# A mixed mLSTM and attention layer on one core: the last normalisation as weighted rows with a shift from row-group products, and a third block of rows as row products

## The chip, the cores and the metric

The kernel is one program on one core of a Trainium2 chip. The metric is the device time of one execution in microseconds (us), the median of three runs. Engines are TensorE (PE; its loads of stationary operands are PEld), VectorE (DVE), ScalarE (ACT), GpSimd (POOL) and SyncE (SP, which issues nearly all DMAs here). SBUF is the memory the engines work on, PSUM the one that TensorE writes its sums to.

## What is computed

One inference step of a hybrid decoder layer, for 512 prompt tokens and 32 sample tokens (8 sequences of 4), 2048 wide. Only its end is touched: the output projection, the residual and the normalisation.

```python
def _layernorm(x, w, b):
    xf = x.astype(jnp.float32)
    mu = jnp.mean(xf, axis=-1, keepdims=True)
    var = jnp.mean(jnp.square(xf - mu), axis=-1, keepdims=True)
    return (xf - mu) * lax.rsqrt(var + LN_EPS) * w.astype(jnp.float32) + b.astype(jnp.float32)
...
    y = (jax.nn.sigmoid(g_m) * jnp.einsum('btc,cd->btd', br_m, w_proj_m)
         + jax.nn.sigmoid(g_a) * jnp.einsum('btc,cd->btd', br_a, w_proj_a))
    out = jnp.einsum('btc,cd->btd', y, w_out)
    return _layernorm(DN_ALPHA * x + out, ln_w, ln_b).astype(x.dtype)
```

## The kernel before

Input projection, attention, the mLSTM state updates and two inner projections come first and take some 2285 us; nothing of them is changed. All products are made of values split in two (`hilo`, `split`: a rounded high part on ScalarE, the rest on VectorE), three products for each pair: high by high, low by high, high by low.

The last stage multiplies the gated sum `y` (tiles `yh`, `yl`, 2048 rows by T = 544 tokens) with `w_out`. Weight columns go in 16 groups `ct` of 128. For groups 0 to 12 the weights are the stationary operand and the tokens stream through: 16 inner steps x 3 products x two pieces of 256 and 288 tokens. The result stands transposed, columns by tokens; ScalarE copies it to `ot` (`evac`), TensorE turns it back in pieces of 128 tokens (`add_residual`, by `ident`), and VectorE adds it to `z`, which holds the prompt's rows as 4 blocks of 128 tokens (`zs` holds the 32 sample rows, folded to 128 partitions by 512). After each fourth group, `stats` collects mean and variance of a quarter of each row (`bn_stats`).

For the last three groups (`G3 = 3`, 13 to 15) only tokens 256 to 543 are done that way: 48 products of 288 columns each. For token blocks 0 and 1 the roles are swapped in `rows_of(t)`: the tokens of the block are the stationary operand, the 384 weight columns stream through in pieces of 256 and 128, 96 products a block, and the sum comes out as rows, so that one operation of VectorE (`add_rows`, L1692) adds them, with no transpose behind.

`moments(t)` makes a block's mean and variance, and GpSimd raises the variance to the power -1/2 (L1660). `finish(t)` then works in pieces: VectorE makes (z - mean) x `lw` (L1677); either VectorE makes that times the power plus `lb` (L1682), or ScalarE multiplies and GpSimd adds (L1679, L1680); SP sends the piece out. Blocks 2 and 3 and the samples are finished beside `rows_of(0)`, block 0 beside `rows_of(1)`, block 1 last in smaller pieces (`LAST`). `load_ln` loads `ln_w` and `ln_b`, each copied to all 128 partitions, and in the samples' folded form (`lwq`, `lbq`: the 32 partitions of row group q hold quarter q).

The instructions of an engine run in the order of its queue. A scheduler with its own model of times sets this order from the program, ahead of time; where `manual_schedule` names TensorE, its instructions stay in the order in which the code issues them. Elsewhere in the kernel there is already a product on four row groups: in the state update (L1133) four products of 32 rows, each with its own `tile_position`, follow one another, and VectorE reads the four results (L1136). fp32 products, as with `ident` or `cq`, run at full precision.

## Time and profile before

| | us |
|---|---|
| median of 3 runs | 2511.45 (2511.23 to 2512.54) |
| profiled execution | 2510.62 |
| its span | 2508.8 |
| TensorE busy | 2468.9 (98%) |
| VectorE busy | 1778.4 (71%) |
| ScalarE busy | 1211.9 (48%) |
| GpSimd busy | 366.5 (15%) |

The profile shows one execution. Its page gives the busy time of each engine and the chain of work that ended last (TensorE makes up 89% of it); the trace behind it gives every instruction with start and duration. Products on TensorE are pipelined, so that the duration of one overlaps the next: the price of one in a row of them is the distance between starts.

### The profile page before, as it was taken

How to read it: one execution, taken by the hardware profiler on the slowest of the kernel's cores; microseconds unless marked ns; L12 is line 12 of the kernel's file. 1: busy time of each engine (PE TensorE's matmuls, PEld its weight loads, DVE VectorE, ACT ScalarE, POOL GpSimd, SP SyncE). 2: the span in 40 equal slices, each digit the busy share in tenths (PEclk: the TensorE clock that was granted, in tenths of full speed). 3: DMA queues.
4: the chain of work that ended last, by engine and by line, in shares of the span. 5: the costliest groups of instructions: out<-in, count | busy, mean ns of one | idle time of the engine just before them, and what ended most of it. 6: DMA issues, size and time to landing. Idle time of an engine off the chain costs nothing.

```text
span 2508.8 us, 48732 instructions
## 1 busy us (share of the span) xinstructions
PE 2468.9 (98%) x19711; PEld 2408.4 (96%) x19711; DVE 1778.4 (71%) x2608; ACT 1211.9 (48%) x1965; POOL 366.5 (15%) x442
## 2 busy tenths in 40 slices
PE   8999999999999999999999999999999999999997
PEld 8999999999999999999999999999999998999997
DVE  7867777777777777788777888877766655766336
ACT  4447667667667665433434445444533323344221
POOL 2111111111111111221111222100000011110002
PEclk9999999999999999999999999999999999999998
DMA  6566666666666655477585784874555467987332
GB/s 194 136 167 149 160 157 153 152 153 156 150 158 152 153 135 152 118 245 238 168 276 170 233 251 131 260 239 128 180 167 164 163 207 218 249 207 236 93 102 80
DMA packets 548322, 439.18 MB, mean 175 GB/s; under 512 B 44256, under 2 KB 459280, under 8 KB 547808
## 3 DMA queue, kind: packets, MB, share of 16 engines
q1 hardware_dynamic: 535392, 389.85, 52.8%
q0 software_dynamic: 12704, 46.21, 10.0%
q8 instruction: 155, 2.54, 0.4%
q14 instruction: 71, 0.58, 0.1%
HBM read 302.68 MB, written 90.32 MB: 157 GB/s over the span
## 4 chain that ended last, share of the span: by engine, by line
PE 89%; DMA 3%; DVE 2%; issue 1%; ACT 1%; SPq 0%; POOL 0%; DVEq 0%; ACTq 0%; POOLq 0%
PE bank L634 43%; PE bank L636 21%; PE bank L229 11%; PE sm L1317 2%; PE sum L1128 1%; PE sm L1349 1%; PE sm L1362 1%; PE sm L744 1%; PE sm L784 1%; PE bank L1727 1%; PE sm L774 1%; PE sm L229 1%; DMA d_n<-fr 1%; PE sm L1133 1%; DVE wl L213 1%
## 5 line engine op out<-in xcount | busy, mean ns | idle before, releaser
L212 ACT CAST wh<-raw 128x1024 fp32r<-128x1024 f32 x628 | 657.8, 1048 | 889.1 <-PE bank L634 595.2
L213 DVE TENSOR_TENSOR wl<-raw,wh 128x1024 fp32r<-128x1024 f32 x628 | 778.5, 1242 | 296.2 <-ACT wh L212 293.2
L634 PE MATMUL bank<-xk,wh 128*128 128x272 f32 x2304 | 315.9, 289 | 1.7 <-DVE ev L659 1.7
L614 DVE TENSOR_TENSOR raw<-raw,raw 128x1024 f32<-128x1024 f32 x234 | 297.9, 1273 | 25.4 <-DMA raw<-in_w_proj_m 17.1
L634 PEld LDWEIGHTS bank<-xk,wh 128*128 128x128 f32 x2304 | 297.8, 188 | 5.3 <-issue 2.5
L653 POOL TENSOR_TENSOR ev<-p,ev 128x272 f32<-128x272 f32 x80 | 115.1, 1439 | 564.0 <-ACT ev L652 530.2
L636 PE MATMUL bank<-xk,wl 128*128 128x272 f32 x1152 | 167.1, 287 | 0.0
L636 PEld LDWEIGHTS bank<-xk,wl 128*128 128x128 f32 x1152 | 153.5, 188 | 0.0
L634 PE MATMUL bank<-n2h,wh 128*128 128x272 f32 x576 | 147.3, 289 | 2.0 <-ACT wh L212 2.0
L634 PE MATMUL bank<-s4h,wh 128*128 128x272 f32 x576 | 148.7, 291 | 0.0
L634 PE MATMUL bank<-s1h,wh 128*128 128x272 f32 x576 | 148.7, 291 | 0.1
L634 PE MATMUL bank<-a11h,wh 128*128 128x272 f32 x576 | 148.0, 289 | 0.0
L634 PE MATMUL bank<-n3h,wh 128*128 128x272 f32 x576 | 147.5, 289 | 0.0
L634 PE MATMUL bank<-a11l,wh 128*128 128x272 f32 x576 | 147.2, 289 | 0.0
L634 PE MATMUL bank<-n3l,wh 128*128 128x272 f32 x576 | 146.9, 288 | 0.0
L634 PE MATMUL bank<-s4l,wh 128*128 128x272 f32 x576 | 146.7, 287 | 0.0
L634 PE MATMUL bank<-s1l,wh 128*128 128x272 f32 x576 | 146.6, 287 | 0.0
L634 PE MATMUL bank<-n2l,wh 128*128 128x272 f32 x576 | 146.6, 287 | 0.0
L612 POOL DMA_DIRECT2D raw<-raw x86 | 74.5, 866 | 403.5 <-DVE raw L614 173.7
L659 DVE SCALAR_TENSOR_TENSOR ev<-bank,ev 128x272 f32<-128x272 f32 x80 | 35.3, 441 | 119.4 <-PE bank L636 119.4
L229 PE MATMUL bank<-bh,wl 128*128 128x272 f32 x512 | 109.9, 291 | 6.3 <-DVE wl L213 6.3
L634 PEld LDWEIGHTS bank<-n2h,wh 128*128 128x128 f32 x576 | 108.3, 188 | 3.2 <-ACT wh L212 2.2
(503 smaller groups left out, 5928.9 us busy)
## 6 DMA issues: line engine op xcount, KB each, us to landing
raw<-in_w_in SPq DMA_DIRECT2D x296, 512.0 KB
raw<-raw POOLq DMA_DIRECT2D x86, 512.0 KB, 4.9
C<-in_state_mlstm_C SPq DMA_DIRECT2D x32, 1024.0 KB
out<-C SPq DMA_DIRECT2D x64, 512.0 KB
raw<-in_w_proj_a SPq DMA_DIRECT2D x32, 512.0 KB
raw<-in_w_proj_m SPq DMA_DIRECT2D x32, 512.0 KB
raw<-in_w_out SPq DMA_DIRECT2D x32, 512.0 KB
d_sgm<-ev SPq DMA_DIRECT2D x16, 272.0 KB
```

The lines of the kernel that those rows point to most:

```text
L212: state["wh"] = A.copy(wh[:], raw[:])
L213: state["wl"] = V.tensor_tensor(out=wl[:], in0=raw[:], in1=r32(wh[:]), op=ALU.subtract)
L229: PE.matmul(ps[ALL, f, 0:w], a[:, kk], b(k, c, w), start=(k == 0 and n == 0), stop=(k == 15 and n == 2))
L612: G.dma_start(out=w[out][:], in_=w[b][:], accum_op=ALU.add)
L614: V.tensor_tensor(out=w[out][:], in0=w[a][:], in1=w[b][:], op=ALU.add)
L634: PE.matmul(ps, wh[:, k], x(p, k), start=(first and k == 0 and p == 0), stop=False, skip_group_check=True)
L636: PE.matmul(ps, wl[:, k], x(0, k), start=False, stop=(k == 7), skip_group_check=True)
L653: G.tensor_tensor(out=c22, in0=p1, in1=c11, op=ALU.subtract)
L659: V.scalar_tensor_tensor(c22, B0, -sc, c22, op0=ALU.mult, op1=ALU.add)
L744: PE.matmul(pp[:, c0 + w0:c0 + 256], qs[a][:, j * 128:j * 128 + 128], kx[:, k0:k0 + 256 - w0], start=(n == 0), stop=(n == 1))
L774: PE.transpose(pt[:, (m - m0_) * 128:(m - m0_) * 128 + 128], s_[:, b, 128:256] if own else s_[:, b + 1, 0:128], ident)
L1317: PE.matmul(pp[:, 0:258], a[:, b * 128:b * 128 + 128], b_[:, b, f], start=(b == 0 and n == 0), stop=(b == 3 and n == 2))
```

## The change

The normalisation is rearranged: (z - m) r w + b becomes (z w) r + (b - m r w). The first factor, z w, is made ahead (`weighted`): for the first three quarters of each row as soon as their statistics are taken, for the last quarter of a block behind its statistics. The second term, the shift, is a product with five inner rows: `sh` holds, for each quarter on its own 32 partitions, the high and low parts of b and w (rows 0 to 4: b high, b low, w high, w low, w high), and `mc` holds 1, 1, and the high, high and low parts of -m r. `shift` fills `mc` for a block on VectorE, `turned` transposes it on TensorE and copies it on ScalarE, and `finish` makes four products of 32 rows by 512 columns, one on each row group, into four banks. VectorE then makes z r + shift, one operation for each quarter. For the very last quarter TensorE adds z r itself by a product with a diagonal matrix of r (`dg`, fp32), and ScalarE copies the result out. `lb` and its 1 MB load are gone; GpSimd keeps only the power.

Block 2 moves to the row products as well: `rows_of` runs for blocks 2, 0 and 1, and the last three groups do 160 columns (block 3 and the samples) in place of 288. The row products and what is put between them (`at2`, `at8`, ...: the inner step ahead of which it is issued) are in program order on TensorE.

```diff
 SLOPES = [float(np.float32(2.0 ** (-8.0 * (h + 1) / AH))) for h in range(AH)]
-C_ID, C_TRI, C_DIST, C_SB, C_M8, C_SM, C_SEL, C_R, C_Q, C_N = 0, 128, 256, 512, 644, 652, 684, 716, 730, 858
+C_ID, C_TRI, C_DIST, C_SB, C_M8, C_SM, C_SEL, C_R, C_Q, C_N = 0, 128, 256, 512, 644, 652, 684, 716, 730, 862
...
     c[:, C_Q:C_Q + 128] = np.where(tok[:, None] == tok[None, :], 0.25, 0.0)
+    j = p % 32
+    for n, rows in enumerate(((0, 1), (2, 3, 4), (0, 2, 4), (1, 3))):
+        c[:, C_Q + 128 + n] = np.isin(j, rows)
...
     lw = d1.tile([128, D], F32, name="lw")
-    lb = d1.tile([128, D], F32, name="lb")
+    sh = d1.tile([128, 512], F32R, name="sh")
+    shw = [d1.tile([128, 512], F32, name=nm("shw")) for _ in range(2)]
+    mc = [d1.tile([128, 4, 32], F32R, name=nm("mc")) for _ in range(2)]
+    mT = [d1.tile([128, 128], F32R, name=nm("mT")) for _ in range(2)]
+    mr = d1.tile([128, 4], F32, name="mr")
+    dg = d1.tile([128, 128], F32, name="dg")
...
         nc.sync.dma_start(z[:, :, cs], xrows[:, :, cs])
         nc.sync.dma_start(zs[r], xs_src[:, cs])
-    cq = d1.tile([128, 128], F32, name="cq")
+    cq = d1.tile([128, 132], F32, name="cq")
     def load_ln():
-        nc.sync.dma_start(cq[:], i["consts"][:, C_Q:C_Q + 128])
+        nc.sync.dma_start(cq[:], i["consts"][:, C_Q:C_Q + 132])
         nc.sync.dma_start(lw[:], i["ln_w"].partition_broadcast(128))
-        nc.sync.dma_start(lb[:], i["ln_b"].partition_broadcast(128))
...
             nc.sync.dma_start(lbq[r], i["ln_b"][cs].partition_broadcast(32))
+    def weighted(lo, hi, c4):
+        cs = slice(c4 * 512, c4 * 512 + 512)
+        V.tensor_tensor(out=z[:, lo:hi, cs], in0=z[:, lo:hi, cs], in1=lw[:, cs].unsqueeze(1).to_broadcast([128, hi - lo, 512]),
+                        op=ALU.mult)
+    def weights_ahead():
+        x_, l_ = shw[0][:], shw[1][:]
+        k = [cq[:, 128 + n:129 + n] for n in range(4)]
+        V.tensor_scalar(x_, lbq, k[0], None, op0=ALU.mult)
+        V.scalar_tensor_tensor(x_, lwq, k[1], x_, op0=ALU.mult, op1=ALU.add)
+        hilo(x_, sh[:], l_)
+        yield
+        V.tensor_scalar(x_, r32(sh[:]), k[2], None, op0=ALU.mult)
+        V.scalar_tensor_tensor(sh[:], l_, k[3], x_, op0=ALU.mult, op1=ALU.add)
+        for n in range(2):
+            V.tensor_scalar(mc[n][:].rearrange("p q x -> p (q x)"), cq[:, 0:128], 0.0, 1.0, op0=ALU.mult, op1=ALU.add)
+        yield
+        for c4 in range(2):
+            for lo in (0, 2):
+                weighted(lo, lo + 2, c4)
+                yield
...
             stats(0, 4, ct // 4)
+            if ct == 11:
+                for lo in (0, 2):
+                    yield
+                    weighted(lo, lo + 2, 2)
...
             pm = sm()
-            PE.matmul(pm[:, 0:2], cq[:], m[:, 0:2], start=True, stop=True)
+            PE.matmul(pm[:, 0:2], cq[:, 0:128], m[:, 0:2], start=True, stop=True)
...
         G.tensor_tensor(out=m[:, 2:3], in0=m[:, 1:2], in1=mh[:, 0:1], op=ALU.pow)
-    CHUNKS = ((1280, 2048, True), (0, 1280, False))
-    LAST = ((1280, 1664, True), (1664, 2048, True), (0, 896, False), (896, 1280, False))
-    def finish(t, chunks=CHUNKS):
-        m, r_ = mv[:, t, 0:1], mv[:, t, 2:3]
-        if t == 4:
-            V.scalar_tensor_tensor(zs, zs, m, lwq, op0=ALU.subtract, op1=ALU.mult)
-            V.scalar_tensor_tensor(zs, zs, r_, lbq, op0=ALU.mult, op1=ALU.add)
-            for q in range(4):
-                nc.sync.dma_start(ys_rows[:, q * 512:q * 512 + 512], zs[q * 32:q * 32 + 32])
-            return
+    def shift(t):
+        m, r_, n = mv[:, t, 0:1], mv[:, t, 2:3], t in (1, 2)
+        V.scalar_tensor_tensor(mr[:, t:t + 1], m, -1.0, r_, op0=ALU.mult, op1=ALU.mult)
+        hi = mc[n][:, :, 2:4]
+        V.tensor_copy(hi, mr[:, t:t + 1].unsqueeze(2).to_broadcast([128, 4, 2]))
+        V.tensor_tensor(out=mc[n][:, :, 4:5], in0=mr[:, t:t + 1].unsqueeze(2).to_broadcast([128, 4, 1]),
+                        in1=r32(mc[n][:, :, 2:3]), op=ALU.subtract)
+    def turned(t):
+        n = t in (1, 2)
+        pt = sm()
+        PE.transpose(pt[:, 0:128], r32(mc[n][:]).rearrange("p q x -> p (q x)"), ident)
+        A.copy(mT[n][:], pt[:, 0:128])
+    def finish(t):
+        r_, n = mv[:, t, 2:3], t in (1, 2)
         dst = y_p[0, t * 128:t * 128 + 128, :]
-        for c0, c1, on_pool in chunks:
-            c = slice(c0, c1)
-            zt = z[:, t, c]
-            V.scalar_tensor_tensor(zt, zt, m, lw[:, c], op0=ALU.subtract, op1=ALU.mult)
-            if on_pool:
-                A.activation(zt, zt, AF.Copy, scale=r_)
-                G.tensor_tensor(out=zt, in0=zt, in1=lb[:, c], op=ALU.add)
+        if t == 1:
+            A.activation(dg[:], ident, AF.Copy, scale=r_)
+        for q in range(4):
+            rows_, cs = slice(q * 32, q * 32 + 32), slice(q * 512, q * 512 + 512)
+            ps = bank()
+            scaled = (t, q) == (1, 3)
+            PE.matmul(ps[:], mT[n][rows_], sh[rows_], start=True, stop=not scaled, tile_position=(q * 32, 0), skip_group_check=True)
+            if scaled:
+                PE.matmul(ps[:], dg[:], z[:, t, cs], start=False, stop=True, skip_group_check=True)
+                A.copy(z[:, t, cs], ps[:])
             else:
-                V.scalar_tensor_tensor(zt, zt, r_, lb[:, c], op0=ALU.mult, op1=ALU.add)
-            nc.sync.dma_start(dst[:, c], zt)
+                V.scalar_tensor_tensor(z[:, t, cs], z[:, t, cs], r_, ps[:], op0=ALU.mult, op1=ALU.add)
+            if t == 1 or q % 2:
+                c = cs if t == 1 else slice(q * 512 - 512, q * 512 + 512)
+                nc.sync.dma_start(dst[:, c], z[:, t, c])
+    def finish_samples():
+        m, r_ = mv[:, 4, 0:1], mv[:, 4, 2:3]
+        V.scalar_tensor_tensor(zs, zs, m, lwq, op0=ALU.subtract, op1=ALU.mult)
+        V.scalar_tensor_tensor(zs, zs, r_, lbq, op0=ALU.mult, op1=ALU.add)
+        for q in range(4):
+            nc.sync.dma_start(ys_rows[:, q * 512:q * 512 + 512], zs[q * 32:q * 32 + 32])
     def tail_task(ct, ot):
-        add_residual(ct, ot, 2, 5)
+        add_residual(ct, ot, 3, 5)
...
         moments(t)
+        weighted(t, t + 1, 3)
+        shift(t)
     rows = {}
-    def rows_of(t, meanwhile):
+    def rows_of(t, **meanwhile):
         ps = rows[t] = sm()
         for k in range(KT):
-            if k == 2:
-                meanwhile()
+            if f"at{k}" in meanwhile:
+                meanwhile[f"at{k}"]()
...
                 load_ln()
+            elif ct == 11:
+                spawn(weights_ahead())
...
                 wh, wl = w1[half]
-            products(ps[:].unsqueeze(1), half, wh, wl, yh, yl, ((0, 256, 288),))
+            products(ps[:].unsqueeze(1), half, wh, wl, yh, yl, ((0, 384, 160),))
         ot = ev()
-        A.copy(ot[:, 256:T], ps[:, 0:288])
+        A.copy(ot[:, 384:T], ps[:, 0:160])
         if g < G3 - 1:
             spawn(tail_task(ct, ot))
-    rows_of(0, lambda: (add_residual(15, ot, 2, 5), stats(2, 4, 3), [moments(t) for t in (2, 3, 4)], finish(2), finish(3), finish(4)))
-    rows_of(1, lambda: (add_rows(0), finish(0)))
-    add_rows(1)
-    finish(1, LAST)
     drain()
+    with tc.manual_schedule(engines={PE.engine}):
+        rows_of(2, at2=lambda: (add_residual(15, ot, 3, 5), stats(3, 4, 3), moments(3), weighted(3, 4, 3), shift(3)),
+                at8=lambda: moments(4), at11=lambda: turned(3), at14=lambda: finish(3))
+        rows_of(0, at1=lambda: add_rows(2), at4=lambda: finish_samples(), at9=lambda: turned(2), at12=lambda: finish(2))
+        rows_of(1, at1=lambda: add_rows(0), at9=lambda: turned(0), at12=lambda: finish(0))
+        add_rows(1)
+        turned(1)
+        finish(1)
```

TensorE at its end. Before, the last row products (here L1708, six to an inner step; `w_*` hold the columns of groups 13 and 14, `wh`, `wl` those of 15) are the last instructions:

```order
L1708 MATMUL sm_29065<-w_3775_28719,yh_27074 128x256
L1708 MATMUL sm_29065<-wl_28895,yh_27074 128x128
L1708 MATMUL sm_29065<-w_3774_28718,yl_27075 128x256
L1708 MATMUL sm_29065<-wh_28894,yl_27075 128x128
L1797 UNCONDITIONAL_BRANCH
```

Now (row products are L1762 there), the transpose of `mc`, the four products on row groups and the diagonal product follow:

```order
L1762 MATMUL sm_29211<-w_3780_28735,yl_27075 128x256
L1762 MATMUL sm_29211<-wh_28913,yl_27075 128x128
L1708 MATMUL sm_29343<-cc,mc_27108 128x128
L1720 MATMUL bank_29347<-sh,mT_27110 128x512
L1720 MATMUL bank_29351<-sh,mT_27110 128x512
L1720 MATMUL bank_29355<-sh,mT_27110 128x512
L1720 MATMUL bank_29359<-sh,mT_27110 128x512
L1722 MATMUL bank_29359<-z,dg 128x512
```

The transpose and four such products also stand once inside the row products of block 2, of block 0 and of block 1, for the block before.

VectorE at its end, before, for block 1 (residual, statistics, variance, then the pieces):

```order
L1692 SCALAR_TENSOR_TENSOR z<-z,sm_29065 128x384
L1633 BN_STATS stt<-z 128x6
L1649 BN_AGGR mv<-stt 128x2
L1650 TENSOR_SCALAR mv<-mv 128x1
L1677 SCALAR_TENSOR_TENSOR z<-z,mv,lw 128x384 x2
L1677 SCALAR_TENSOR_TENSOR z<-z,mv,lw 128x896
L1677 SCALAR_TENSOR_TENSOR z<-z,mv,lw 128x384
L1682 SCALAR_TENSOR_TENSOR z<-z,mv,lb 128x896
L1682 SCALAR_TENSOR_TENSOR z<-z,mv,lb 128x384
```

Now, for the same block:

```order
L1744 SCALAR_TENSOR_TENSOR z<-z,sm_29211 128x384
L1663 BN_STATS stt<-z 128x6
L1683 BN_AGGR mv<-stt 128x2
L1621 TENSOR_TENSOR z<-z,lw 128x512
L1684 TENSOR_SCALAR mv<-mv 128x1
L1699 SCALAR_TENSOR_TENSOR mr<-mv 128x1
L1701 CAST mc_27108<-mr 128x4x2
L1702 TENSOR_TENSOR mc_27108<-mr,mc_27108 128x4
L1725 SCALAR_TENSOR_TENSOR z<-z,mv,bank_29347 128x512
L1725 SCALAR_TENSOR_TENSOR z<-z,mv,bank_29351 128x512
L1725 SCALAR_TENSOR_TENSOR z<-z,mv,bank_29355 128x512
```

The weighting of the last quarter (L1621) stands ahead of the variance, the small operations of the shift come behind it, and three operations read the banks.

VectorE early in the stage, now (L216 is the split's low part, L1651 and L1658 the residual; before, only these stand there):

```order
L216 TENSOR_TENSOR wl_27239<-raw_27134,wh_27238 128x1024
L1635 TENSOR_SCALAR mc_27107<-cq 128x128
L1635 TENSOR_SCALAR mc_27108<-cq 128x128
L216 TENSOR_TENSOR wl_27351<-raw_27344,wh_27350 128x1024
L1651 SCALAR_TENSOR_TENSOR z<-z,sm_27402 128x4x128
L1658 SCALAR_TENSOR_TENSOR zs_27113<-zs_27113,sm_27408 32x128
L216 TENSOR_TENSOR wl_27421<-raw_27346,wh_27420 128x1024
L1628 TENSOR_SCALAR shw_27105<-zs_27115,cq 128x512
L1629 SCALAR_TENSOR_TENSOR shw_27105<-zs_27114,cq,shw_27105 128x512
L269 TENSOR_TENSOR shw_27106<-shw_27105,sh 128x512
L1632 TENSOR_SCALAR shw_27105<-sh,cq 128x512
```

The fills of `mc` and the making of `sh` have come in between the splits; the first needs the constants `cq`, the second the folded rows of `ln_b` and `ln_w` (their tiles are named `zs` too).

## Rows read from the trace of the kernel before

**Rows 1.** Busy time by stretch: us, engines, granted clock, DMA share, GB/s.

```profile
core 0: us, PE busy (x) PEld busy (x) DVE busy (x) ACT busy (x) POOL busy (x), PEclk, DMA share, GB/s
2490.00:2495.00 5.00, 3.84 (x34) 3.70 (x33) 4.97 (x8) 0.94 (x1) 3.53 (x3) 1.00 0.25 95
2495.00:2500.00 5.00, 0.00 (x0) 0.00 (x0) 4.90 (x8) 0.52 (x2) 1.34 (x2) 0.60 0.68 252
2500.00:2505.00 5.00, 0.00 (x0) 0.00 (x0) 4.22 (x4) 0.60 (x2) 2.58 (x2) 0.50 0.30 116
```

**Rows 2.** Chain of waits from 2440 us: start, us, what.

```profile
2445.06 5.99 PE bank L229 x48
...
2454.88 0.44 PE sm L1620 x4
...
2461.45 6.36 PE sm L229 x48
...
2474.31 0.42 DVE z L1621
```

**Rows 3.** Timeline of TensorE, row products: start, us, engine, line, operation, out<-in.

```profile
2482.64 0.33 PE L1708 MATMUL sm<-w,yh 128*128 128x256 f32 x1
...
2492.99 0.33 PE L1708 MATMUL sm<-w,yh 128*128 128x256 f32 x1
...
2493.62 0.22 PE L1708 MATMUL sm<-wh,yl 128*128 128x128 f32 x1
```

**Rows 4.** Timeline of all engines from 2496 us.

```profile
2496.76 0.54 DVE L1692 SCALAR_TENSOR_TENSOR z<-z,sm 128x384 f32<-128x384 f32 x1
...
2498.59 0.85 POOL L1660 TENSOR_TENSOR mv<-mv,mh 128x1 f32<-128x1 f32 x1 [3.10 <-DVE mv L1650]
...
2501.82 2.40 DVE L1682 SCALAR_TENSOR_TENSOR z<-z,mv,lb 128x896 f32<-128x896 f32 x2
```

**Rows 5.** Timeline of TensorE around products of 64 columns (L940).

```profile
1022.36 1.89 PE L940 MATMUL sm<-turned,vb 128*128 128x64 f32 x16
1024.06 0.37 PE L634 MATMUL bank<-n3h,wh 128*128 128x272 f32 x1
1024.27 0.29 PE L634 MATMUL bank<-n3l,wh 128*128 128x272 f32 x1
```

**Rows 6.** Chain of waits around products on four row groups (L1133).

```profile
1098.85 2.00 PE bank L634 x16
...
1102.84 0.44 PE sm L1133 x3
1103.28 2.21 PE bank L634 x16
```

**Rows 7.** Groups by form, whole span: count | busy us, mean ns | idle before.

```profile
L1136 DVE SCALAR_TENSOR_TENSOR C<-C,dcb,sm 128x512 f32<-128x512 f32 x128 | 87.7, 740 | 0.9
...
L965 DVE SCALAR_TENSOR_TENSOR lns<-lns 128x1 f32<-128x1 f32 x16 | 2.5, 157 | 0.4
...
L963 POOL TENSOR_TENSOR lns<-lns,mh 128x1 f32<-128x1 f32 x16 | 8.8, 550 | 236.2 <-DVE lns L956 154.9 <-DVE lns L957 44.0 <-DVE lns L962 37.4
...
L265 ACT CAST a21h<-sm 128x128 fp32r<-128x128 f32 x2 | 0.5, 272 | 0.3 <-PE sm L323 0.3
...
L498 ACT COPY ev<-sm 128x512 f32<-128x512 f32 x2 | 1.2, 586 | 2.7 <-PE sm L494 2.7
```

**Rows 8.** Busy time by stretch, early in the last stage (columns as in rows 1).

```profile
2300.00:2305.00 5.00, 5.00 (x42) 5.00 (x41) 1.22 (x1) 1.05 (x1) 0.00 (x0) 1.00 1.03 347
...
2340.00:2360.00 20.00, 20.00 (x164) 19.98 (x163) 8.21 (x12) 3.72 (x5) 0.00 (x0) 1.00 0.28 79
```

**Rows 9.** Timelines of SP, VectorE and ScalarE early in the last stage.

```profile
2316.44 0.31 SPq L1610 DMA_DIRECT2D zs<-in_ln_b  x1
...
2321.09 1.23 DVE L213 TENSOR_TENSOR wl<-raw,wh 128x1024 fp32r<-128x1024 f32 x1 [0.50 <-ACT wh L212]
...
2325.56 1.05 ACT L212 CAST wh<-raw 128x1024 fp32r<-128x1024 f32 x1 [4.50 <-PE bank L229]
```

**Rows 10.** Timeline of TensorE: one fp32 product of 512 columns, two records.

```profile
1180.65 1.05 PE L1082 MATMUL sm<-w,cc 128*32 128x512 f32 x2
```

## What I predicted before the run

> **What bounds the kernel now.** I read the page first, then the last 40 us in the table of stretches, the chain of waits, and the timelines of the engines there. Outside the output projection and the normalisation every engine's instructions keep their order, so the sum is made after 2451 us, with a look at the early part of this stage for new waits. The table of stretches [rows 1] shows three regimes. Past 2490 us TensorE still has no gap (3.84 us of that stretch, all of it up to its last product), at the full granted clock. From 2490 to 2500 us VectorE is full as well (4.97 and 4.90 of 5). After that there is only a tail. The chain of waits [rows 2] says the same: the products of weight columns 13, 14 and 15 follow column 12 on TensorE from 2451.05 us (48 products of 288 columns in 6.36 us), then the chain steps over to VectorE at 2474.31 us and stays there to the end.
>
> Two points matter. TensorE's last row product starts at 2493.62 us and lasts 0.22 [rows 3], so TensorE ends at E = 2493.84 us, and the span at 2508.8: a tail of 14.96 us. VectorE reaches the first instruction that needs those products (L1692) only at 2496.76 us [rows 4], 2.9 us after E, because it is behind with the other blocks. Without that backlog the tail would be 12.0 us. So the change can win a few microseconds in the tail, and whatever it adds to TensorE before E is paid in full.
>
> **The change, part by part: TensorE up to E.** (a) Narrower products: 3 columns x 48 products go from 288 to 160. One of 288 takes 6.36/48 = 0.1325 us [rows 2]. One of 160 the trace doesn't show. The lower bound is by columns alone: 128 columns fewer at the full 2.4 GHz level are 0.053 us, which leaves 0.079. The upper bound is a narrow product with the same 128x128 stationary operand: 16 products of 64 columns run from 1022.36 to the next start at 1024.06 us, 0.106 us each, or 0.111 if the start behind that (1024.27, one ordinary step of 0.125 later) is taken for the end [rows 5]. That is four times what 64 columns need. Something that does not shrink with the columns, most likely the load of the stationary operand, sets a floor, and 160 columns need less than this floor; I take 0.108. Gain: 144 x 0.0245 = 3.5 us; by columns 7.7. Each column also loses one transpose of 0.11 us (four take 0.44 [rows 2]): 0.33 us.
>
> The Trainium skill, page "TensorE: Matmul & The Clock Gate", section "Back-to-back issue gap", gives about 81 ns to a product of 128 columns in a stream of loads and products. The row of 64 columns speaks against it; by the page's figure (a) would gain an estimated 144 x (0.1325 - 0.081) = 7.4 us.
>
> (b) The third block of rows: 96 products more. Six go to each step of the inner dimension; from 2482.64 to 2492.99 us there are 15 steps [rows 3], 0.69 us each, so a block's 16 cost 11.0 us. Shapes and order are those of the two blocks before, so this needs no bounds. Here the move loses: the columns that go (144 x 128) equal those that come (48 x 384), but those that go barely shorten a product, and those that come are new products, two to each operand.
>
> (c) The shift: for three of the four blocks, four products of 32 rows by 512 columns on four row groups stand between row products. The state update has just this: four of them take 0.44 us in the chain, and the 16 ordinary products behind them 2.21 instead of 2.00 us [rows 6], 0.65 us a set. 3 x 0.65 = 1.95 us, and 3 transposes, 0.33. One after another, 512 columns at 2.4 GHz each, a set would be 0.86 + 0.21 us.
>
> The Trainium skill, page "TensorEngine Tiling (Array Packing)", section "Key Properties", says that a change of tiling mode drains TensorE. The 0.21 us behind a set is where the row would show it; a drain of that length ahead of each set too would be an estimated 0.6 us in all.
>
> E: -3.5 - 0.33 + 11.0 + 1.95 + 0.33 = +9.5 us, to 2503.3 us.
>
> **Does TensorE wait inside the row products?** They now stand in program order, so a late shift of block 2 holds all that is behind it. VectorE first finishes block 3: four operations at 0.69 us (L1136 has this shape, with its product in PSUM, 87.7 us for 128 [rows 7]), 2.8 us. Then block 2's residual, statistics, weighting and shift, 3.9 us (as in the tail below, with 0.85 for the power). TensorE meanwhile has two steps left and nine more, 7.6 us. The margin is 0.9 us; for block 0, with 4 + 9 steps, 2.3 us. I take no wait; a chain longer by 2 us would make one of about 1 us.
>
> **Earlier in the stage.** VectorE gets four operations for the shift's rows and six weightings of 128x1024, about 1.2 us each, where it is busy 8.21 of 20 us [rows 8], and TensorE has no gap. GpSimd and SP lose work there. But VectorE now waits for small DMAs: first for the constants of the two `mc` fills, which are issued ahead of all the rows, then for the rows of ln_b (last issue 2316.44 us [rows 9]). Behind the second wait stand five operations (about 3 us) and the split that starts at 2321.09 us now and feeds TensorE at about 2325.5, when the column before ends [rows 9]. The 1 MB broadcast of ln_b that stood ahead of those transfers is gone, some 3 us at the 347 GB/s of that stretch [rows 8]. I cost this at nothing: rows that land at 2319 us give a split at 2322 to 2323. If they land at 2322, TensorE waits about 1 us.
>
> **The tail after E.** From the start of L1692 to the end of GpSimd's power are 2499.44 - 2496.76 = 2.68 us [rows 4]. VectorE's queue now has the weighting (0.62 us, half of a 128x1024) between the aggregate and the variance, and GpSimd's power no longer meets two-operand work of VectorE (0.85 us here, 0.55 in the mean of L963 [rows 7]): 3.0 us. Three tiny VectorE operations of 0.16 [rows 7], 0.5 us; the transpose, about 0.45, and ScalarE's copy of 128, 0.27 [rows 7]: 0.75. Then four row-group products and the diagonal one. TensorE has by then been idle for 4 us, and the granted clock stands at its lower level in the stretches behind 2500 us (0.50, after a mean of 0.60 over 2495 to 2500) [rows 1]. So I double the full-clock values: 0.44 becomes 0.9, and an fp32 product of 512 columns, two records of together 1.05 us [rows 10], becomes 2.1. ScalarE's copy of 512 is 0.59 [rows 7]: 3.6 us. VectorE's three operations, 2.1 us from the first product on, end sooner. From the last producer to the end of the span were 2508.8 - 2504.22 = 4.58 us [rows 4]; with 256 instead of 192 KB, 4.7. Tail: 0.05 + 3.0 + 0.5 + 0.75 + 3.6 + 4.7 = 12.6 us, 2.4 less. At the full clock the tail would be 1 us shorter; two hand-overs more of 0.2 us make it longer by 0.4.
>
> **Sum.** +9.5 - 2.4 = +7.1 us. The profiled execution took 2510.62 us with a span of 2508.8, which becomes 2515.9. The median of the runs is 2511.45, 0.83 above it: I forecast 2518.6 us.
>
> **Rivals.** First, products by columns: at 0.079 us for 160 columns E comes 4.2 us sooner, and the time is 2514.4 us, inside what can't be told from no change. For it: in pairs of 256 and 288 columns the mean is 0.125 (48 in 5.99 us [rows 2]), so width does count there. Against it: the 64-column row. It decides at 0.093 us per product: below that the change isn't slower by over 0.2%. With the skill's 81 ns the time would be an estimated 2514.7 us.
>
> Second, TensorE waits: the 0.9 us of block 2 fail, or the split behind the ln_b rows comes late. Each costs 1 to 2 us on top: 2520 to 2521 us. For it: 0.9 us is small against a chain of nine hand-overs.
>
> Third, the row groups don't overlap among row products as they do in the state update, and the change doesn't do what it says: three sets of 0.86 instead of 0.44, and the one at the lower clock twice as much, 2 us more, 2520.7 us. Against it: rows 6 are the same operation.
>
> **How the numbers follow.** Forecast 0.62, products by columns 0.15, waits 0.14, no overlap 0.05; 0.04 is left for a faster kernel, for which no row gives a mechanism. A measurement of this kernel can't tell about 0.2%, 5 us, from no change: 2506.4 to 2516.5. The forecast lies 2.1 us above that, and with a tail 2 us shorter it falls inside; 0.09 of its 0.62 go there. Same: 0.15 + 0.09 = 0.24; slower: 0.53 + 0.14 + 0.05 = 0.72; faster 0.04. The range goes from 2513.0 (by columns, and a tail 1.4 us shorter) to 2522.7 (waits and no overlap together).
>
> **What would show it.** In the profile of the changed kernel: 48 products of 160 columns in 5.2 us (right) or 3.8 (by columns); 0.65 us for each set of row groups; no idle time of TensorE between 2451 and 2503 us; VectorE at the last rows within 0.1 us of the last row product; the diagonal product at the lower clock and ScalarE's copy as the last producer. The forecast is wrong if TensorE's last row product ends before 2500 us, or the tail is under 11 us.

## The result, and the profile after

| | kernel before | changed kernel |
|---|---|---|
| median of the runs, us | 2511.88 (2509.35 to 2513.7, 12 runs) | 2517.43 (2515.06 to 2520.65, 12 runs) |
| profiled execution, us | 2510.62 | 2516.07 |
| its span, us | 2508.8 | 2514.3 |
| end of weight column 12 (C), us | 2451.05 | 2450.91 |
| end of the last row product (E), us | 2493.84 | 2503.34 |
| tail, from E to the end of the span, us | 14.96 | 10.96 |

The change makes the kernel slower by a quarter of a per cent: the ratio is 1.0025, with a 95% interval from 1.0016 to 1.0033. The forecast was 2518.6 us.

The table of stretches of the changed kernel, in the columns of [rows 1], shows the same regimes moved: TensorE is full until E, now past 2500 us, and VectorE, which had 4.2 to 5 us of work in each of these stretches, has 0.10 us of work in the last full stretch ahead of E.

```profile
2490.00:2495.00 5.00, 5.00 (x46) 5.00 (x46) 4.01 (x11) 0.00 (x0) 0.55 (x1) 1.00 0.53 210
2495.00:2500.00 5.00, 5.00 (x49) 4.92 (x47) 0.10 (x1) 0.27 (x1) 0.00 (x0) 1.00 0.02 3
2500.00:2505.00 5.00, 3.35 (x29) 2.95 (x28) 4.27 (x8) 0.00 (x0) 0.00 (x0) 1.00 0.46 181
2505.00:2510.00 5.00, 2.74 (x7) 0.97 (x7) 2.50 (x8) 0.67 (x2) 0.55 (x1) 0.59 0.08 30
```

The chain of waits of the changed kernel (start, us, what), against [rows 2] and [rows 6]. The first row gives C. The second is a column's 48 products, 160 columns wide now: 0.111 us each, where 288 columns took 0.1325. The third is one set of row-group products among row products, 0.43 us. Behind it 66 products, 11 steps of 0.69, take 7.75 instead of 7.59 us, so a set costs 0.59.

```profile
2450.91 3.43 PE sm L232 x31
...
2459.66 5.33 PE sm L232 x48
...
2477.99 0.43 PE bank L1720 x2
2478.41 7.75 PE sm L1762 x66
```

The timeline of the tail in the changed kernel (start, us, engine, line, operation, in the brackets the wait ahead of it), against [rows 3] and [rows 4]. L1744 is what L1692 was. It starts 0.04 us behind E, not 2.9; GpSimd's power takes 0.55 us, not 0.85; and the last producer is ScalarE's copy behind the diagonal product (L1722), which takes 2.08 us.

```profile
2503.12 0.22 PE L1762 MATMUL sm<-wh,yl 128*128 128x128 f32 x1
...
2503.38 0.55 DVE L1744 SCALAR_TENSOR_TENSOR z<-z,sm 128x384 f32<-128x384 f32 x1 [0.20 <-PE sm L1762]
...
2505.64 0.55 POOL L1694 TENSOR_TENSOR mv<-mv,mh 128x1 f32<-128x1 f32 x1 [11.15 <-DVE mv L1684]
...
2506.62 0.17 DVE L1702 TENSOR_TENSOR mc<-mr,mc 128x4 fp32r<-128x4 f32 x1
...
2507.42 0.27 ACT L1709 CAST mT<-sm 128x128 fp32r<-128x128 f32 x1 [0.79 <-PE sm L1708]
...
2508.47 2.08 PE L1722 MATMUL bank<-z,dg 128*128 128x512 f32 x2
2508.57 2.06 DVE L1725 SCALAR_TENSOR_TENSOR z<-z,mv,bank 128x512 f32<-128x512 f32 x3 [1.77 <-PE bank L1720]
2510.58 0.58 ACT L1723 COPY z<-bank 128x512 f32<-128x512 f32 x1 [2.90 <-PE bank L1722]
```

The list of TensorE's waits in the changed kernel, from 2440 us on (what waited for what: us in total, times, longest). Both are in the tail; between the row products there is none.

```profile
PE sm L1708 <- DVE mc L1702: 3.5, 1, 3.5
PE bank L1720 <- ACT mT L1709: 0.4, 1, 0.4
```

### The profile page after: what moved, and what is told of

Same layout as the page of the kernel before. It is cut to its first block, busy times and chain, and to the rows that moved or that the text cites. A ratio compares the mean times of both kernels' runs of the same rounds, so it can differ in the third digit from the quotient of the medians.

```text
span 2514.3 us, 48986 instructions
## 1 busy us (share of the span) xinstructions
PE 2479.4 (99%) x19826; PEld 2415.7 (96%) x19826; DVE 1780.8 (71%) x2638; ACT 1210.5 (48%) x1967; POOL 354.5 (14%) x437
## 4 chain that ended last, share of the span: by engine, by line
PE 91%; DMA 2%; DVE 1%; issue 1%; ACT 1%; SPq 0%; POOLq 0%; POOL 0%; DVEq 0%; ACTq 0%
PE bank L637 43%; PE bank L639 21%; PE bank L232 12%; PE sm L1320 2%; PE sum L1131 1%; PE sm L1352 1%; PE sm L1365 1%; PE sm L747 1%; PE sm L787 1%; PE sm L777 1%; PE bank L1781 1%; PE sm L1762 1%; PE sm L232 1%; DMA raw<-in_w_in 1%; PE sm L1136 1%
## 5 line engine op out<-in xcount | busy, mean ns | idle before, releaser
L216 DVE TENSOR_TENSOR wl<-raw,wh 128x1024 fp32r<-128x1024 f32 x628 | 779.0, 1242 | 281.0 <-ACT wh L215 278.4
```

The source lines that it names most:

```text
L216: state["wl"] = V.tensor_tensor(out=wl[:], in0=raw[:], in1=r32(wh[:]), op=ALU.subtract)
```

## The experiments

What is done up to weight column 12 hardly differs between the kernels, and yet C lies between 2450.5 and 2454.5 us in their profiled executions. Spans of single executions therefore say little about 2 us. I count from C: the stage from C to E, and the tail behind it, repeat to 0.1 us where a kernel does the same work. The runs e3b, e5, e7 and e8 are one execution each (2559.13, 2518.47, 2518.19 and 2517.59 us), on another chip than e1, e2, e4, e6 and e9, where the kernel before took 2514.29 us once. They too are read from C on.

| kernel | C | E | C to E | tail | C to the end |
|---|---|---|---|---|---|
| before | 2451.05 | 2493.84 | 42.79 | 14.96 | 57.75 |
| changed | 2450.91 | 2503.34 | 52.43 | 10.96 | 63.39 |
| e1, two blocks | 2454.53 | 2500.06 | 45.53 | 10.74 | 56.27 |
| e2, third block alone | 2453.08 | 2503.54 | 50.46 | 12.06 | 62.52 |
| e4, one of 384 | 2451.78 | 2499.39 | 47.61 | 10.91 | 58.52 |
| e3b, two of 80 | 2450.47 | 2546.53 | 96.06 | 10.87 | 106.93 |
| e5, no diagonal | 2453.29 | 2505.73 | 52.44 | 10.97 | 63.41 |
| e7, clock kept | 2453.39 | 2505.82 | 52.43 | 10.58 | 63.01 |
| e8, one transfer | 2451.89 | 2504.33 | 52.44 | 11.47 | 63.91 |
| e6, together | 2452.71 | 2495.70 | 42.99 | 11.10 | 54.09 |
| e9, with GpSimd | 2453.72 | 2497.39 | 43.67 | 11.11 | 54.78 |

My theory was that of the prediction: TensorE sets E, the third block of rows is what costs, because a narrow product costs nearly as much as a wide one, and the new normalisation itself gains a little in the tail.

**The third block undone, e1.**

```diff
-            products(ps[:].unsqueeze(1), half, wh, wl, yh, yl, ((0, 384, 160),))
+            products(ps[:].unsqueeze(1), half, wh, wl, yh, yl, ((0, 256, 288),))
...
-        rows_of(2, at2=lambda: (add_residual(15, ot, 3, 5), stats(3, 4, 3), moments(3), weighted(3, 4, 3), shift(3)),
-                at8=lambda: moments(4), at11=lambda: turned(3), at14=lambda: finish(3))
+        rows_of(0, at2=lambda: (add_residual(15, ot, 2, 5), stats(2, 4, 3), moments(2), moments(3), weighted(2, 4, 3), shift(2), shift(3)),
+                at10=lambda: moments(4), at13=lambda: (turned(2), turned(3)), at15=lambda: finish(2))
...
```

> The change with one part undone: block 2 goes back into the weight columns 13 to 15 (products of 288 columns), so two blocks are computed as rows, and blocks 2 and 3 are normalised together. My theory (the third block is what costs; a product of 160 columns is hardly shorter than one of 288): 96 products less, -11.0 us, 144 products wider again by 0.1325 - 0.111 us, +3.1 us. TensorE's last row product ends at 2503.3 - 7.9 = 2495.4 us, the tail stays at 11 to 12 us, the span is 2506.5 to 2507.5, about 1.5 us below before and 7 below the changed kernel. Rival (what costs is the normalisation in program order, the third block is paid back by its narrower products): the end stays at 2502 us or later, the span at 2513 or more. Rival (VectorE's backlog of 2.9 us returns with the third block gone): the end at 2495.4, but a tail of 14 us, span 2509.5.

Measured: 2510.33 us (median of 10), ratio to before 0.9993, interval 0.9984 to 1.0002. From C to the end it takes 56.27 us, 1.48 less than before (expected: about 1.5) and 7.12 less than the changed kernel (expected: 7). Chain of waits of e1, a column's 48 products at 288 columns again, and C:

```profile
2454.53 3.86 PE sm L232 x29
...
2465.00 6.40 PE sm L232 x48
```

C to E is 6.9 us shorter than in the changed kernel, where I expected 7.9. Three transposes of 0.11 us that come back with the wider columns were left out of that sum, and TensorE waits 0.4 us for a shift; that is 0.7 of the missing 1.0. The tail is 10.74 us: VectorE's backlog doesn't return. So the normalisation by weighted rows and a shift is by itself a small gain (1.5 us from C on; the interval of the whole times doesn't exclude zero), and the third block turns it into a loss.

**The third block alone, e2.** The edit is the opposite one, in the kernel before:

```diff
-            products(ps[:].unsqueeze(1), half, wh, wl, yh, yl, ((0, 256, 288),))
+            products(ps[:].unsqueeze(1), half, wh, wl, yh, yl, ((0, 384, 160),))
...
-    rows_of(0, lambda: (add_residual(15, ot, 2, 5), stats(2, 4, 3), [moments(t) for t in (2, 3, 4)], finish(2), finish(3), finish(4)))
+    rows_of(2, lambda: (add_residual(15, ot, 3, 5), stats(3, 4, 3), [moments(t) for t in (3, 4)], finish(3), finish(4)))
+    rows_of(0, lambda: (add_rows(2), finish(2)))
```

> The kernel before with the third block of rows alone: columns 13 to 15 with products of 160, rows of the blocks 2, 0 and 1, the old normalisation. My theory: TensorE's last row product ends at 2493.8 + 11.0 - 3.1 - 0.3 = 2501.4 us; VectorE's backlog of 2.9 us goes, since it has 11 us more, and the tail is 12.0: a span of 2513.4, 4.6 us above before and 0.9 below the changed kernel. Rival (the columns set a product's price): the end at 2497.2, a span of 2509. Rival (the backlog comes from the old normalisation, not from too little time): a tail of 15 us, a span of 2516.

Measured: 2517.18 us (median of 10), ratio 1.0022, interval 1.0012 to 1.0031. C to E grows by 7.67 us, expected 7.6; the tail is 12.06, expected 12.0; together 4.77 us more than before, expected 4.6. Here the last row product of e2 in its timeline, and in its chain the first instruction of VectorE behind it:

```profile
2503.32 0.22 PE L1708 MATMUL sm<-wh,yl 128*128 128x128 f32 x1
```

```profile
2503.58 0.57 DVE z L1692
```

VectorE starts 0.04 us behind E. The backlog of 2.9 us goes with the third block alone, without the new normalisation: E comes 7.67 us later, and VectorE was behind by less. Beside the third block the new normalisation is no gain: the changed kernel takes 63.39 us from C to the end, e2 62.52.

**The floor of a product, e3b.**

`halves` is `products` with two pieces to each operand.

```diff
-            products(ps[:].unsqueeze(1), half, wh, wl, yh, yl, ((0, 384, 160),))
+            halves(ps[:, 0:160].rearrange("p (f x) -> p f x", f=2), half, wh, wl, yh, yl, ((0, 384, 80), (1, 464, 80)))
```

> The changed kernel with each of the 144 products of 160 columns as two of 80, so the columns stay and the loads of the stationary operand double. My theory (a floor of about 0.11 us per product that doesn't shrink with the columns): 144 x 0.11 = +15.9 us, 96 products in 10.6 us per column, and a span of 2530. Rival (the price goes by columns, with about 0.012 us per product beside them): +1.7 us, a span of 2516.

Measured: a span of 2557.4 us, and 96.06 us from C to E, 43.6 more than in the changed kernel, against 15.9 by my theory and 1.7 by the rival. Two things happen. The timeline of e3b shows one step of six products of 80 columns from 2453.35 to 2454.02 us, 0.112 us each. Then the table of stretches (columns of [rows 1]) shows the granted clock fall to its lower level, while TensorE has no gap before or behind, and the chain shows 96 products in 20.33 us, 0.212 each.

```profile
2453.35 0.62 PE L242 MATMUL sm<-yh,w 128*128 128x80 f32 x4
...
2454.02 0.62 PE L242 MATMUL sm<-yh,w 128*128 128x80 f32 x4
```

```profile
2453.00:2454.00 1.00, 1.00 (x11) 1.00 (x11) 1.00 (x2) 0.00 (x0) 0.00 (x0) 1.00 0.00 0
2454.00:2455.00 1.00, 1.00 (x10) 1.00 (x9) 0.74 (x1) 0.00 (x0) 0.00 (x0) 0.85 0.06 16
2455.00:2456.00 1.00, 1.00 (x7) 1.00 (x6) 0.00 (x0) 0.00 (x0) 0.00 (x0) 0.50 0.00 0
```

```profile
2457.73 20.33 PE sm L242 x96
```

The floor is as expected: 80 columns take 0.112 us where 160 took 0.111; at half the clock it is 0.212, nearly twice as much. The floor accounts for 15.9 of the 43.6 us; the other 27.7 are the lower clock, which I had not foreseen. Products by columns are out.

The Trainium skill, page "TensorE: Matmul & The Clock Gate", section "Back-to-back issue gap", gives about 81 ns for 128 columns in a stream of loads and products. In these rows, with operands of type fp32r, 80 columns take 112 ns at the full clock, so here the page's figure doesn't hold, and the measurement decides.

**Fewer loads for the same columns, e4.** Two thirds of the row products, those with the high part of the weights, become one product.

```diff
-                for c, w, b in ((0, 256, w2[k // 8][p][:, k % 8].rearrange("p g c -> p (g c)")),
-                                (256, 128, w1[k // 8][p][:, k % 8])):
+                b = w2[k // 8][p][:, k % 8].rearrange("p g c -> p (g c)")
+                for c, w, b in ((0, 384, b),) if p == 0 else ((0, 256, b), (256, 128, w1[k // 8][:, k % 8])):
...
```

> The changed kernel with two thirds of the row products (those with the high part of the weights) as one product of 384 columns instead of one of 256 and one of 128; the columns stay, the loads of the stationary operand fall by a third of what the rows had. My theory (the 128 columns pay the floor of 0.11 us, and would need 0.053 by columns): 32 pairs of 0.229 us become 32 products of 384 / 2.4 GHz = 0.160 to 0.172 us, -1.8 to -2.2 us a block, -5.5 to -6.6 us in three blocks: TensorE's last row product ends at 2496.8 to 2497.8 us, and with a tail of 11 the span is 2508 to 2509, or up to 2 us more if VectorE falls behind. Rival (the price goes by columns): no change, 2514.

Measured: 2512.29 us (median of 10), ratio to before 1.0004, interval 0.9994 to 1.0013. C to E is 4.8 us shorter than in the changed kernel (expected: 5.5 to 6.6), and VectorE doesn't fall behind. In the timeline of e4 a step goes from 2497.27 to 2497.84 us: 0.57 instead of 0.69. The mean step is 0.58, and from C to E the 96 products saved give 0.05 us each.

```profile
2497.27 0.39 PE L1762 MATMUL sm<-w,yl 128*128 128x384 f32 x1
2497.49 0.45 PE L1762 MATMUL sm<-w,yh 128*128 128x384 f32 x2
2497.78 0.22 PE L1762 MATMUL sm<-wl,yh 128*128 128x128 f32 x1
2497.84 0.39 PE L1762 MATMUL sm<-w,yl 128*128 128x384 f32 x1
```

The columns are the same, the products and their loads a third fewer, and the time falls: a row block pays by the product. Every product here has a load of its own, so no run parts the load from any other fixed price of a product; that the load is the floor stays argued.

**The diagonal product taken away, e5.** VectorE finishes the last quarter too.

```diff
-        if t == 1:
-            A.activation(dg[:], ident, AF.Copy, scale=r_)
...
-            scaled = (t, q) == (1, 3)
+            scaled = False
```

> The changed kernel without the diagonal product: VectorE takes the last quarter too. In the changed kernel VectorE needs 0.69 us for a quarter from 0.1 us behind the first product on, and ScalarE's copy ends 2.7 us behind that start because the diagonal product runs at the lower clock (2.08 us). My theory: four quarters on VectorE end after 2.75 us, the tail is the same within 0.2 us (10.9 to 11.2). Rival (the diagonal product saves VectorE's quarter, 0.69 us): a tail of 11.6.

Measured: a tail of 10.97 us, against 10.96 with it. The timeline of e5:

```profile
2510.95 2.72 DVE L1723 SCALAR_TENSOR_TENSOR z<-z,mv,bank 128x512 f32<-128x512 f32 x4 [1.77 <-PE bank L1718]
```

Four quarters on VectorE end 2.72 us behind its start; with the diagonal product ScalarE's copy ended 2.59 behind that start, and from the last producer to the end of the span it took 3.14 us, 3.03 here. At the lower clock the diagonal product is worth nothing.

**TensorE kept at work in the tail, e7.**

```diff
         add_rows(1)
+        busy = sm()
+        for _ in range(28):
+            PE.transpose(busy[:, 0:128], ident, ident)
         turned(1)
```

> The changed kernel with 28 transposes of no use (0.11 us each, 3.1 us) between TensorE's last row product and the last block's transpose, where it is idle for 3.5 us. My theory (the 2.08 us of the diagonal product are the lower clock, and this clock comes from the idle time): granted clock 1.0 up to the diagonal product, which takes 1.05 us; VectorE's third quarter is then the last producer, and the tail is 10.96 - 0.7 = 10.2 to 10.3 us. Rival (an fp32 product of 512 columns takes 2.08 us here at any clock, or the clock falls in spite of the work): 10.96, or longer by what the transposes hold up.

Measured: a tail of 10.58 us, 0.38 less, where I expected 0.7. The mechanism is right. Timeline and stretches of e7: the diagonal product takes 1.12 us at a granted clock of 1.00, and VectorE's third quarter is the last producer.

```profile
2510.56 1.12 PE L1722 MATMUL bank<-z,dg 128*128 128x512 f32 x2
2510.66 2.06 DVE L1725 SCALAR_TENSOR_TENSOR z<-z,mv,bank 128x512 f32<-128x512 f32 x3 [1.39 <-PE bank L1720]
2511.73 0.58 ACT L1723 COPY z<-bank 128x512 f32<-128x512 f32 x1 [1.65 <-PE bank L1722]
```

```profile
2510.00:2512.00 2.00, 1.56 (x6) 0.49 (x6) 1.33 (x3) 0.35 (x2) 0.00 (x0) 1.00 0.00 0
```

But from the last producer (2512.72 us) to the end of the span there are now 3.68 us, not 3.14: four quarters of 256 KB are done within 1.4 us, faster than they can be written (some 385 GB/s in the last stretches of this trace). Behind the last producer 858 KB are left to write instead of 660, and the last bytes move 2.44 us behind it instead of 1.90. What the engines win, the transfers take back in part.

**The last two quarters in one transfer, e8.**

```diff
-            if t == 1 or q % 2:
-                c = cs if t == 1 else slice(q * 512 - 512, q * 512 + 512)
+            if (t == 1 and q < 2) or q % 2:
+                c = cs if t == 1 and q < 2 else slice(q * 512 - 512, q * 512 + 512)
```

> The changed kernel with the last two quarters of the last block written by one transfer of 512 KB instead of two of 256 KB, issued when the last of them is done. The time from the last producer to the end of the span was 3.14 us here and 4.58 in the kernel before, where 640 KB were issued in its last 0.9 us. My theory (the bytes that are still to be moved when the last transfer is issued make the difference, at some 386 GB/s): 256 KB more, +0.68 us, 3.8 us. Rival (the length of the end goes with the engines that close the program, GpSimd's work above all): 3.1 us.

Measured: the last producer ends at 2511.56 + 0.58 = 2512.14 us, the span at 2515.8: 3.66 us (expected: 3.8; by the rival 3.1), and a tail longer by 0.51. The timeline of e8:

```profile
2511.56 0.58 ACT L1723 COPY z<-bank 128x512 f32<-128x512 f32 x1 [2.89 <-PE bank L1722]
```

The size is near the forecast, but the reason is another one. Behind the last producer 660 KB are written in both kernels. In e8 the last transfer is issued at 2512.17 us, too late to follow what is under way: nothing is written from 2512.60 to 2512.90, and the last bytes move 2.30 us behind the last producer instead of 1.90. Nor is the rival out for the kernel before: in e8 GpSimd's work is that of the changed kernel. Where the 4.58 us of the kernel before come from is read from the traces, in the next section.

**Together, e6 and e9.** e6 takes two blocks (e1), the wide products (e4) and the busy TensorE (e7); block 2's chain stands ahead of block 3's, and the weighting of the last quarter behind the variance. e9 moves three of these weightings from VectorE to GpSimd.

```diff
...
-        weighted(t, t + 1, 3)
+        with behind("eps"):
+            weighted(t, t + 1, 3)
...
```

> What the runs so far point to, together: two blocks of rows, two thirds of the row products as one of 384 columns, TensorE kept at work with 28 transposes ahead of the last shift, and VectorE's weighting of the last quarter behind the variance instead of ahead of it; block 2's chain stands ahead of block 3's. Counted from the end of weight column 12, the two-block kernel took 45.5 us to TensorE's last row product and a tail of 10.7. My theory: -3.5 us for the 64 products saved, -0.8 for the waits, so 41.3; the tail -0.4 for the clock and -0.5 for the variance, plus the backlog of VectorE, which now has two blocks of some 9.3 us for 19 us of work: 0 to 2 us. Together 51.5 to 53.5 us against 57.75 in the kernel before: 4 to 6 us faster than it (ratio 0.9975 to 0.9983), 10 to 12 faster than the changed kernel. Rival (VectorE is the bound in the row blocks): the tail is over 13 us and the gain under 3.5 us.

> The same kernel, with the weighting of the last quarter of the blocks 2, 3 and 0 on GpSimd, behind the power: 3 x 0.55 us less on VectorE. If VectorE is the bound in the row blocks and GpSimd doesn't slow it, the tail is up to 1.6 us shorter. Rival (two-operand work on both engines slows both, as in the kernel before, where the power took 0.85 us and not 0.55 beside VectorE's work): VectorE's operations beside GpSimd's get longer by what is won, or GpSimd is late, and the time is the same or longer.

Measured for e6: 2507.9 us (median of 11), ratio to before 0.9982, interval 0.9974 to 0.9991; from C to the end 54.09 us, 3.66 less than before and 9.3 less than the changed kernel. I expected 51.5 to 53.5, so 0.6 to 2.6 us are missing. C to E is 42.99 instead of 41.3: TensorE waits 0.7 us for block 2's shift, I had taken 0.8 off for waits that had cost 0.4 in e1, and 64 products at the 0.05 us of e4 save 3.2, not 3.5; the last 0.3 us I can't place. VectorE starts on the last rows 0.7 us behind E. And moving the weighting gained nothing, as the timeline of e6 shows:

```profile
2496.40 0.55 DVE L1744 SCALAR_TENSOR_TENSOR z<-z,sm 128x384 f32<-128x384 f32 x1
...
2498.08 0.68 DVE L1621 TENSOR_TENSOR z<-z,lw 128x512 f32<-128x512 f32 x1
...
2498.24 0.92 POOL L1694 TENSOR_TENSOR mv<-mv,mh 128x1 f32<-128x1 f32 x1 [7.33 <-DVE mv L1684]
```

GpSimd's power now runs beside VectorE's two-operand weighting and takes 0.92 instead of 0.55 us. From the start of L1744 to the end of the power are 2.76 us, against 2.81 in the changed kernel.

Measured for e9: 2508.87 us (median of 11), ratio 0.9984, interval 0.9975 to 0.9993: no gain over e6. GpSimd's weighting takes 1.27 us, and a VectorE operation on one column, started 0.05 us behind it, ends with it, after 1.24 us instead of 0.16. Two timelines of e9, GpSimd's and VectorE's:

```profile
2478.46 1.27 POOL L1621 TENSOR_TENSOR z<-z,lw 128x512 f32<-128x512 f32 x1
```

```profile
2478.51 1.24 DVE L1699 SCALAR_TENSOR_TENSOR mr<-mv 128x1 f32<-128x1 f32 x1
```

That is the rival. The Trainium skill, page "SBUF — State Buffer", section "SBUF: two separate sides", says that an operation of VectorE with two inputs in SBUF and an operation of GpSimd that reads SBUF share a pair of ports as an exclusive lock, held for a whole instruction. The 1.24 us agree: both inputs of that operation are in SBUF.

## Why the prediction was right, step by step

**TensorE up to E** was forecast at +9.5 us. From C to E it is +9.64. That E itself came at 2503.34, with 2503.3 forecast, is luck in part: C, which scatters by 4 us, lay within 0.14 us in these two executions.

- Narrower products: forecast 0.108 us each and -3.5 us, measured 0.111 and 144 x 0.0215 = -3.1. The floor that I took from a product of 64 columns [rows 5] holds for 160 columns and, by e3b, for 80. It was the step on which the sign rested; the first rival, 0.079 us, is out.
- The third block: forecast 11.0 us. e2 gives 7.67 + 3.1 + 0.33 = 11.1.
- Row-group sets: forecast 0.65 us each, measured 0.59. Some 0.1 us of this lie ahead of the first of the four products and 0.05 behind the last. They overlap among row products as they did in the state update [rows 6]; the third rival is out.
- Waits: none, as forecast. Block 2's shift was ready 1.5 us ahead of its transpose (forecast 0.9), block 0's 2.6 us (forecast 2.3). The margin was real but thin: in e6, with steps of 0.57 us, a like chain does hold TensorE, for 0.7 us. The waits of VectorE for small transfers early in the stage made no new gap on TensorE, and left C where it was.

**The tail** was forecast at 12.6 us and came at 10.96, just under the 11 us that I had named as the point where the forecast fails. By that sign the forecast of the tail failed; the total held, since C to E was right within 0.2 us. In the order of the forecast the terms came at 0.04 (0.05), 2.81 (3.0), 0.60 (0.5), 0.90 (0.75), 3.47 (3.6) and 3.14 (4.7). The last one is the term that was mis-sized: I took the 4.58 us from the last producer to the end over from the kernel before, with 0.1 more for a larger last piece, as if the length belonged to the program.

It is not the bytes. Behind the last producer 640 KB were written in the kernel before and 660 in the changed one. The two traces part the difference of 1.44 us in four (e2, with the old normalisation, agrees with the kernel before in each):

- The last bytes move 2.15 us behind the last producer before, with a pause of 0.28 us on the way, 1.90 now: 0.25.
- The landing of the last transfer is reported 0.71 us behind its last bytes before, 0.34 now: 0.37. Why, no run shows.
- SP waits for the transfers' semaphores one after another, 0.06 us each. Before, that of the last transfer stood near the head of this row, now at its end: 0.57 us from the landing to SP's DRAIN (one of the instructions that close the program on each engine), 0.14 now: 0.43.
- GpSimd's DRAIN ends 5.28 us behind GpSimd's last operation, in each of the eleven traces here. In the kernel before, GpSimd adds `lb` until 2502.75 us, so its DRAIN, 7.38 us long, ends at 2508.02, and its next step comes 0.42 us behind SP's DRAIN. In the changed kernel its last operation is the power, its DRAIN is over at 2511.47, and the step follows SP's DRAIN by 0.03: 0.39.

The closing instructions, those of the kernel before first (line, engine, operation, count: least, median and longest in ns, first and last start in us):

```profile
L1797 POOLq EVENT_SEMAPHORE  x4: 17/17/17, 2508.1 to 2508.7; - x4
L1797 POOLq DRAIN  x3: 40/102/7383, 2500.6 to 2508.5; - x3
L1797 SPq DRAIN  x3: 7/7/7, 2507.6 to 2508.3; - x3
...
L1857 POOLq EVENT_SEMAPHORE  x4: 17/17/17, 2513.6 to 2514.2; - x4
L1857 POOLq DRAIN  x3: 40/93/5862, 2505.6 to 2514.0; - x3
L1857 SPq DRAIN  x3: 7/7/7, 2513.5 to 2513.8; - x3
```

No run changes one of the four alone. That GpSimd's adding leaves the end is part of the new normalisation, so those 0.39 us are a gain of its own, and I had not counted them.

The 1.6 us that this term is off are what parts the forecast span, 2515.9 us, from the 2514.3 measured. The diagonal product at the lower clock, the missing backlog and VectorE's start within 0.1 us of E were as forecast.

What I had not separated is where the tail's gain comes from. By e2 the backlog, 2.9 us of the tail's 4.0, goes with the third block alone, since it delays E by more than VectorE was behind; by e1 it goes without the third block too, with the new normalisation. Either one would have done, and the change pays for both: alone the parts are worth -1.48 us (e1) and +4.77 (e2) from C to the end, together +5.64, not +3.29.

## What to carry to other kernels

Count products before columns: with 80 and 160 columns both at some 0.11 us here, a product narrower than that gains nothing, and moving 128 columns from a product that exists into a new one is a loss even when the columns balance. When an engine's backlog sets the tail, look which part of a change takes it away, and don't pay twice. At the very end, the bytes still to be written when the last producer is done (e7), a pause in the writing (e8) and an engine that closes late (GpSimd, 5.28 us behind its last operation) each cost some tenths of a microsecond: measure the end of the new order, don't carry over that of the old.

## What the chip showed that I had not expected

In e3b the granted clock fell from 1.00 to 0.50 (from 2.4 to 1.2 GHz) in the middle of the first column of 80-column products, with TensorE 1.00 us busy in each microsecond before and behind the fall. It stayed there through the other two columns (25.00 of 25 us busy) and came back among the row products of 256 and 128 columns. Some 58 us at half the clock cost about half of that, the 28 us that the floor leaves over:

```profile
2480.00:2505.00 25.00, 25.00 (x120) 24.94 (x119) 0.57 (x2) 0.29 (x1) 0.00 (x0) 0.50 0.00 1
...
2530.00:2545.00 15.00, 15.00 (x132) 14.36 (x130) 6.68 (x15) 0.27 (x1) 0.55 (x1) 1.00 0.18 71
```

The changed kernel's products of 160 columns, 0.111 us apart, kept the full clock throughout (1.00 in every stretch from 2451 to 2505 us). In the kernel before, the three falls between 30 us and the tail (at 42, 2103 and 2288 us) stand in or just behind gaps of TensorE; this one doesn't. So a busy TensorE is not always a fast one, and in this execution narrow products cost far more than their floor at the full clock. It is one execution; that the narrow products are the cause, and which property of them, no other run shows.
